# A decoder layer with stick-breaking attention: a pair's two heads taken together, K's low products on half of the rows, and two smaller reorderings

## Chip, cores and metric

The kernel runs on one core of a Trainium2 chip. The metric is the device time of one execution in microseconds (us). A core has a tensor engine (PE, whose weight loads are listed apart as PEld), VectorE (DVE), ScalarE (ACT), GpSimd (POOL) and SyncE (SP), which here issues most DMAs.

## The reference, cut to what matters

With a depth of 1 there is one layer: 1024 positions, a width of 1024, 16 heads of 64, everything in 32-bit floats.

```python
def stick_breaking_attention(h, w_in, w_out):
    """A[t,s] = sigmoid(z_ts) * prod_{s<j<t} (1 - sigmoid(z_tj)), s < t."""
    ...
    z = jnp.einsum('bhqd,bhkd->bhqk', qb, k).astype(jnp.float32) * scale
    log_fail = jnp.where(causal, jax.nn.log_sigmoid(-z), 0.0)
    after = lax.cumsum(log_fail, axis=3, reverse=True) - log_fail
    a = jnp.where(causal, jnp.exp(jax.nn.log_sigmoid(z) + after), 0.0)
    return jnp.einsum('bhqk,bhkd->bhqd', a, v.astype(jnp.float32))
    ...

    h = h + stick_breaking_attention(rms_norm(h, norm_mix), sb_w_in, sb_w_out)
    h = h + swiglu(rms_norm(h, norm_ffn), ffn_w_in, ffn_w_out)
    h = h + sigmoid(rms_norm(h, norm_ple) @ ple_w_gate) * (p @ ple_w_proj)
    return rms_norm(h, final_norm)
```

## The kernel before

Activations lie transposed, features on the 128 partitions and positions along the free axis. Every operand of a large product is split into a high part (rounded to the engine's fast 32-bit format) and a low part, the rest; `mm3` (L126) makes three products of 128x128 by 128x512 from them: high by high, high by low, low by high. A weight tile is loaded by SP (`w_load`, L88) and split by `w_split` (L97): ACT copies the high part (L106), DVE or POOL subtracts for the low part (L108). PSUM has eight banks; two (`pj`) belong to projections, the others to the stage at hand.

**Attention** (L169 to L586). The input is loaded, split and squared, and the first pair's Q and K are projected at once (L247 to L264). Then heads go in eight pairs. `proj_steps` (L322) is a generator that yields after each of 48 steps (three matrices, two halves of 512 positions, eight contraction tiles; three products a step) and projects the next pair while the current one is in attention; for the last pair `ple_steps` (L488) takes its place, which projects the embedding and begins the output projection. `evac_q`, `evac_k` and `evac_v` (L278 to L306) empty the projection banks with DVE and ACT. Q of head A lies with its high part on rows 0 to 63 and its low part on rows 64 to 127 (`QA`); head B the other way round (`QB`). K's high part stands on both halves (`KA`, `KB`); its low part (`KLA`, `KLB`) stands on one half beside zeros written once at the start. `evac_v` makes differences of neighbouring positions of V (`dv`, L305), which `turn_v` (L308) transposes on PE; turns wait in the list `late`, which is emptied in the fourth step of each half (L331).

A score atom `s_atom` (L398) is one head and 128 query positions: for each piece of up to 512 key positions (`pieces`, L392) it makes two products into a bank of the tag `zt` (four banks, shared with the transposes), L407 with K's high parts and L408 with its low parts; ACT takes the sigmoid (L410), and DVE a scan over the reversed axis (L417), which is issued behind the next score atom. A value atom `a_atom` (L424) is one head, one window of 512 queries and 128 keys: up to four transposes (L430) into a bank, ACT's high part `ah` (L439), DVE's low part `al` (L440), and, three atoms later (`LAG`), two products with V (L450, L451). `finish` (L457) adds the two halves of the result and, after the second head, V itself, splits it and writes it to DRAM. The loop at L532 lays atoms out by hand: 32 windows (pair, head, half), the score atoms of one window among the value atoms of the window before, and after each atom as many projection steps as a share of weights says (`SHARE`, a score atom weighing `2 * (qt + 1)`). Up to here a planner orders the instructions by dependences, free buffers and the order of issue; from L650 on (`tc_manual`) the order is that of the program. The tag `qf` is a ring of three 512-column buffers for short-lived tiles.

**FFN, first half** (L843 to L914). 22 steps `k`, each with seven products `prod` (a Strassen-like scheme), sums by `add` (L634) that empty the PSUM banks, scaling by the norm (`scaled`, L828, on DVE or POOL) and the gate (`glu`, L830: ACT's sigmoid, then L833 and L834 on DVE, and a DMA to DRAM). `glu` of the second half of the positions is put off to the next step as `tail`. In the last step the first two tiles of the next stage's weights (`w_split(n_fi)`, `w_split(n_fi + 1)`) and activations (`act_split`, L622) are split as well.

**FFN, second half** (L944 to L975). For each half of the positions, 22 steps: eight `mm3`, one into each bank, the first of them into the banks that the sums above have to leave. The gated embedding and the last norm follow.

Of the kernel before, what the change touches and what calls it, by code (L numbers as in the profile page):

```python
# [14 lines left out]
P = 128  # L15
# [10 lines left out]
NA = 4  # L26
SHARE = 0.48
# [13 lines left out]
def tile_trunk(ctx: ExitStack, tc: tile.TileContext, xT, pT, gains, ident, w_qkv, w_o, w_fi, w_fo, w_g, w_p, outT):  # L41
# [54 lines left out]
    def w_split(k):  # L96
        if k < lim[0] and k in raws:  # L97
# [9 lines left out]
            eng = nc.gpsimd if k < N1 or k >= len(order) - 3 else nc.vector  # L107
# [61 lines left out]
    with ExitStack() as c1:  # L169
# [40 lines left out]
        pad = [p1.tile([P, 256], F32R, name=f"pad{k}") for k in range(2)]  # L210
        for k in range(2):
            nc.scalar.copy(pad[k][:, :P], zero)

        VF = [p1.tile([P, T + 1], F32, name=f"vf{q}") for q in range(2)]
        for q in range(2):
            nc.gpsimd.memset(VF[q][:, 0:1], 0.0)

        KLS = [[p1.tile([P, T], F32R, name=f"KL{'AB'[hd]}{q}") for hd in range(2)] for q in range(2)]
        for q in range(2):
            for hd in range(2):  # L220
                r = slice(64 - 64 * hd, 128 - 64 * hd)
                nc.gpsimd.tensor_copy(KLS[q][hd][r, :], zero[r, 0:1].to_broadcast([64, T]))

# [49 lines left out]
        def alloc_qk(pr):  # L273
            for n in ("QA", "QB", "KA", "KB"):
                setattr(prs[pr], n, p1.tile([P, T], F32R, name=f"{n}{pr}", tag=n, bufs=2))
            prs[pr].KL = KLS[pr % 2]

        def evac_q(pr, ps, h):  # L278
            o = prs[pr]
            hs = slice(h * 512, h * 512 + 512)  # L280
            q = p1.tile([P, 512], F32, name="qf", tag="qf", bufs=3)
# [6 lines left out]
        def evac_k(pr, ps, h):  # L288
            o = prs[pr]
            hs = slice(h * 512, h * 512 + 512)  # L290
            q = p1.tile([P, 512], F32, name="kf", tag="qf", bufs=3)
# [5 lines left out]
            nc.gpsimd.tensor_tensor(o.KL[0][0:64, hs], q[0:64], f(o.KA[0:64, hs]), op=ALU.subtract)  # L297
            nc.gpsimd.tensor_tensor(o.KL[1][64:128, hs], q[64:128], f(o.KB[64:128, hs]), op=ALU.subtract)

        def evac_v(pr, ps, h):  # L300
            t0 = h * 512
            v = VF[pr % 2]
            nc.vector.tensor_tensor(v[:, t0 + 1:t0 + 513], ps, rstd[:, t0:t0 + 512], op=ALU.mult)
            dv = p1.tile([P, 512], F32, name="dv", tag="qf", bufs=3)
            nc.vector.tensor_tensor(dv, v[:, t0:t0 + 512], v[:, t0 + 1:t0 + 513], op=ALU.subtract)  # L305
            return dv  # L306
# [15 lines left out]
        def proj_steps(pr, sels=(0, 1, 2)):  # L322
            for sel in sels:
# [38 lines left out]
        def evac_first(h):  # L362
            o = prs[0]
            hs = slice(h * 512, h * 512 + 512)
            q = p1.tile([P, 512], F32, name="qf", tag="qf", bufs=3)
            nc.vector.tensor_tensor(q, qk0[0][h], rstd[:, hs], op=ALU.mult)
            k = p1.tile([P, 512], F32, name="kf", tag="qf", bufs=3)
            nc.vector.tensor_tensor(k, qk0[1][h], rstd[:, hs], op=ALU.mult)
            for hd, (Q, K) in enumerate(((o.QA, o.KA), (o.QB, o.KB))):
# [7 lines left out]
                eng.tensor_tensor(o.KL[hd][a, hs], k[a], f(K[a, hs]), op=ALU.subtract)  # L377
# [20 lines left out]
        def s_atom(pr, hd, qt):  # L398
# [3 lines left out]
            Q = o.QA if hd == 0 else o.QB  # L402
            K = o.KA if hd == 0 else o.KB
            a = p1.tile([P, L], F32, name=f"a{qt}", tag=f"a{qt}", bufs=1)
# [9 lines left out]
            def rest():  # L414

                back = slice(T - 1, T - L - 1 if L < T else None, -1)
                nc.vector.tensor_tensor_scan(a[:, L - 1::-1], a[:, L - 1::-1], hot[:, back], 0.0, op0=ALU.mult, op1=ALU.max)  # L417

            pend_s.append(rest)
            a_tiles[(pr, hd, qt)] = a  # L420
# [3 lines left out]
        def a_atom(pr, hd, w, kt):  # L424
# [6 lines left out]
            c0 = j0 * P  # L431
            if j0 < 3:
                ah = p1.tile([P, 512], F32R, name="ah", tag="ah", bufs=NA)
                al = p1.tile([P, 512], F32R, name="al", tag="al", bufs=NA)
                m0 = c0
            else:
                ah, al = pad
                m0, c0 = P, 256
            nc.scalar.copy(ah[:, m0:m0 + 512 - j0 * P], b[:, j0 * P:])  # L439
            nc.vector.tensor_tensor(al[:, m0:m0 + 512 - j0 * P], b[:, j0 * P:], f(ah[:, m0:m0 + 512 - j0 * P]), op=ALU.subtract)  # L440
            r0 = c0 if j0 < 3 else 0
# [3 lines left out]
            def rest():  # L445
# [4 lines left out]
                nc.tensor.matmul(ps[:, c0:], o.V[:, kt, hd, :], ah[:, r0:], start=kt == 0, stop=False)  # L450
                nc.tensor.matmul(ps[:, c0:], o.V[:, kt, hd, :], al[:, r0:], start=False, stop=last)  # L451
# [5 lines left out]
        def finish(pr, hd, w, ps):  # L457
            if hd == 0:
                stage[(pr, w)] = p1.tile([P, 512], F32, name="stg", tag="stg", bufs=2)
            st = stage[(pr, w)]  # L460
            t = p1.tile([64, 512], F32, name="avt", tag="qf", bufs=3)
            nc.scalar.copy(t, ps[64:128, :])
            nc.vector.tensor_tensor(st[64 * hd:64 * hd + 64, :], ps[0:64, :], t, op=ALU.add)
            if hd == 1:
                ws = slice(w * 512, w * 512 + 512)
                nc.vector.tensor_tensor(st, st, VF[pr % 2][:, w * 512 + 1:w * 512 + 513], op=ALU.add)
                if pr < NPAIR - 1:
                    hl = p1.tile([P, 2, 512], F32R, name="hl", tag="hl", bufs=1)
                    h, l = hl[:, 0, :], hl[:, 1, :]
# [7 lines left out]
                if pr < NPAIR - 1:  # L477
                    nc.sync.dma_start(spill[pr][:, :, ws], f(hl))
# [636 lines left out]
```

## Time and profile before

| | |
|---|---|
| median of 3 runs | 1397.57 us (1396.01 to 1397.66) |
| profiled execution | 1397.2 us, span 1395.4 us |
| PE busy | 1359.3 us, 97% of the span |
| DVE / ACT / POOL busy | 1006.8 / 609.2 / 406.4 us |
| mean granted clock of PE | 0.993 of full speed |

The span reaches from the first to the last instruction; the execution's time has some 2 us around it. Products are pipelined: a product's listed length is a model and longer than the distance to the next one's start, so costs on PE are read from starts. The trace's times count from the span's start.

### The profile page before, as it was taken

To read this page: it belongs to the slowest core of one execution; us is meant where nothing else is said; L and a number is where in the kernel's file an instruction comes from. 1 tells how busy PE (TensorE), PEld (TensorE's weight loads), DVE (VectorE), ACT (ScalarE), POOL (GpSimd) and SP (SyncE) were. 2 spreads that over 40 slices of the span, in tenths; PEclk is the share of its full clock that TensorE was granted. 3 is DMA by queue.
4 is the path that set the end of the run, shared out by engine and by line. 5 is a ranking of instruction groups with operands and counts; after the bars stand their busy time and mean duration, and the time that the engine had idled before them with its cause. 6 is when DMAs were issued, how large, how long until landed. Compare 5 with 4: busy or idle time off the path is not lost. (4 is left out here: it accounts for less than half of the span.)

```text
span 1395.4 us, 17612 instructions
## 1 busy us (share of the span) xinstructions
PE 1359.3 (97%) x6620; PEld 1135.1 (81%) x6620; DVE 1006.8 (72%) x1305; ACT 609.2 (44%) x1082; POOL 406.4 (29%) x280
## 2 busy tenths in 40 slices
PE   8899999999999999999999999999999999999996
PEld 6788888888888878878888888888877888888896
DVE  6778788787887875677888888888884336645775
ACT  6555665655566664443232323222322223433333
POOL 2221322312222501234445444545440000301321
PEclk9999999999999999999999999999999999999998
DMA  5101111111111571442221222221235445555123
GB/s 188 41 31 46 46 46 46 46 34 43 46 46 61 182 263 46 162 146 79 91 85 58 84 91 91 91 71 66 91 106 188 138 156 208 168 175 181 31 71 104
DMA packets 55509, 137.54 MB, mean 99 GB/s; under 512 B 6016, under 2 KB 10496, under 8 KB 55424
## 3 DMA queue, kind: packets, MB, share of 16 engines
q1 hardware_dynamic: 53136, 128.82, 27.1%
q0 software_dynamic: 2016, 7.34, 1.5%
q8 instruction: 52, 0.85, 0.3%
q14 instruction: 33, 0.27, 0.1%
q10 hardware_dynamic: 272, 0.26, 0.1%
HBM read 104.94 MB, written 31.46 MB: 98 GB/s over the span
## 5 line engine op out<-in xcount | busy, mean ns | idle before, releaser
L417 DVE TENSOR_TENSOR_SCAN a<-a,hot 128x128 f32<-128x128 f32 (+7 forms) x128 | 191.7, 1515 | 29.4 <-ACT a L410 28.9
L108 DVE TENSOR_TENSOR wlo<-wraw,whi 128x1024 fp32r<-128x1024 f32 x57 | 71.6, 1256 | 124.4 <-ACT whi L106 124.3
L106 ACT CAST whi<-wraw 128x1024 fp32r<-128x1024 f32 x84 | 88.2, 1051 | 165.2 <-PE b_m L128 144.8
L108 POOL TENSOR_TENSOR wlo<-wraw,whi 128x1024 fp32r<-128x1024 f32 x27 | 67.6, 2509 | 297.6 <-ACT whi L106 141.5
L127 PE MATMUL b_pj<-xh,whi 128*128 128x512 f32 x352 | 141.1, 401 | 0.0
L129 PE MATMUL b_pj<-xh,wlo 128*128 128x512 f32 x352 | 139.1, 395 | 0.4 <-POOL wlo L108 0.4
L128 PE MATMUL b_pj<-xl,whi 128*128 128x512 f32 x352 | 138.5, 393 | 0.0
L440 DVE TENSOR_TENSOR al<-b_tp,ah 128x512 fp32r<-128x512 f32 (+2 forms) x160 | 93.1, 599 | 51.3 <-ACT ah L439 50.9
L439 ACT CAST ah<-b_tp 128x512 fp32r<-128x512 f32 (+2 forms) x160 | 81.9, 522 | 78.4 <-PE b_tp L430 77.5
L410 ACT ACTIVATE a<-b_z 128x128 f32<-128x128 f32 (+2 forms) x192 | 86.8, 490 | 56.5 <-PE b_z L408 55.5
L127 PE MATMUL b_m<-act,whi 128*128 128x512 f32 x264 | 104.0, 394 | 3.5 <-DVE u L634 3.4
L129 PE MATMUL b_m<-act,wlo 128*128 128x512 f32 x264 | 103.8, 393 | 0.2 <-DVE wlo L108 0.2
L128 PE MATMUL b_m<-act,whi 128*128 128x512 f32 x264 | 103.7, 393 | 0.0
L430 PE MATMUL b_tp<-hot,a 128*128 128x128 f32 x576 | 94.2, 272 | 2.6 <-DVE al L440 2.6
L430 PEld LDWEIGHTS b_tp<-hot,a 128*128 128x128 f32 x576 | 72.8, 140 | 25.6 <-DVE al L440 5.6
L129 PEld LDWEIGHTS b_pj<-xh,wlo 128*128 128x128 f32 x352 | 66.3, 188 | 16.3 <-POOL wlo L108 0.5
L128 PEld LDWEIGHTS b_pj<-xl,whi 128*128 128x128 f32 x352 | 66.5, 189 | 9.2
L127 PEld LDWEIGHTS b_pj<-xh,whi 128*128 128x128 f32 x352 | 66.5, 189 | 9.1
L450 PE MATMUL b_av<-ah,V 128*128 128x512 f32 (+2 forms) x160 | 70.7, 442 | 0.0
L941 POOL TENSOR_TENSOR acc<-acc,sq 128x512 f32<-128x512 f32 x10 | 17.6, 1758 | 161.4 <-ACT sq L939 160.7
L832 ACT ACTIVATE sg<-u 128x512 f32<-128x512 f32 x22 | 13.9, 632 | 111.2 <-issue 86.4
L127 PEld LDWEIGHTS b_m<-act,whi 128*128 128x128 f32 x264 | 50.1, 190 | 15.1 <-DVE u L634 4.2
(3039 smaller groups left out, 3746.9 us busy)
## 6 DMA issues: line engine op xcount, KB each, us to landing
fraw<-w_fi SPq DMA_DIRECT2D x44, 512.0 KB, 4.1
wraw<-w_fo SPq DMA_DIRECT2D x44, 512.0 KB, 3.6
wraw<-w_qkv SPq DMA_DIRECT2D x22, 512.0 KB, 3.6
araw<-act SPq DMA_DIRECT2D x44, 256.0 KB, 3.9
h<-h SPq DMA_DIRECT2D x32, 256.0 KB, 3.7
sp<-hl SPq DMA_DIRECT2D x14, 512.0 KB, 3.0
act<-u SPq DMA_DIRECT2D x22, 256.0 KB, 2.2
act<-c SPq DMA_DIRECT2D x22, 256.0 KB, 2.6
```

What stands on the lines that cost most here:

```text
L106: nc.scalar.copy(hi[:, :n, :], t[:, :n, :])
L108: eng.tensor_tensor(lo[:, :n, :], t[:, :n, :], f(hi[:, :n, :]), op=ALU.subtract)
L127: nc.tensor.matmul(ps, whi, xhi, start=first, stop=False)
L128: nc.tensor.matmul(ps, whi, xlo, start=False, stop=False)
L129: nc.tensor.matmul(ps, wlo, xhi, start=False, stop=last)
L410: nc.scalar.activation(a[:, c0:c0 + e], z[:, :e], AF.Sigmoid, scale=-SCALE)
L417: nc.vector.tensor_tensor_scan(a[:, L - 1::-1], a[:, L - 1::-1], hot[:, back], 0.0, op0=ALU.mult, op1=ALU.max)
L430: nc.tensor.transpose(b[:, j * P:(j + 1) * P], a[:, kt * P:(kt + 1) * P], idn)
L439: nc.scalar.copy(ah[:, m0:m0 + 512 - j0 * P], b[:, j0 * P:])
L440: nc.vector.tensor_tensor(al[:, m0:m0 + 512 - j0 * P], b[:, j0 * P:], f(ah[:, m0:m0 + 512 - j0 * P]), op=ALU.subtract)
L450: nc.tensor.matmul(ps[:, c0:], o.V[:, kt, hd, :], ah[:, r0:], start=kt == 0, stop=False)
L941: eng.tensor_tensor(acc3[:, hs], acc3[:, hs], s, op=ALU.add)
```

## The change

**Two heads together.** A score atom now takes both heads of a pair. For each piece it makes both heads' products with K's high parts on all 128 rows, into two banks, and then both heads' products with K's low parts, each on 64 rows only: head A on rows 0 to 63, head B on rows 64 to 127. One tile `KL` per pair holds both low parts without zeros. The two scans of an atom are issued together. There are 16 windows (pair, half) instead of 32, the value atoms of both heads follow each other, and a score atom's weight is `3 * (qt + 1)`. To make room, the zeroed tiles `pad` and `KLS` go (POOL writes zeros beside the last key tile's part instead), V is kept in tiles of 513 columns with a first column that POOL fills, the output's high and low parts pass through the ring `qf`, which has four buffers, and are written by two DMAs instead of one, and the DMA scratch space is cut.

**First pair.** The turns of V of pair 0 are no longer taken up in the first half of the next pair's first matrix.

**Between the FFN's halves.** The low parts of the first two weight tiles of the second half are made on POOL and earlier, and the last step's scaling and gating (now on DVE throughout) is put off until after steps 1 and 2 of the second half.

```diff
+QF = 4
-            eng = nc.gpsimd if k < N1 or k >= len(order) - 3 else nc.vector
+            eng = nc.gpsimd if k < N1 or n_fi <= k < n_fi + 2 or k >= len(order) - 3 else nc.vector
...
-            nc.gpsimd.tensor_tensor(o.KL[0][0:64, hs], q[0:64], f(o.KA[0:64, hs]), op=ALU.subtract)
-            nc.gpsimd.tensor_tensor(o.KL[1][64:128, hs], q[64:128], f(o.KB[64:128, hs]), op=ALU.subtract)
+            nc.gpsimd.tensor_tensor(o.KL[0:64, hs], q[0:64], f(o.KA[0:64, hs]), op=ALU.subtract)
+            nc.gpsimd.tensor_tensor(o.KL[64:128, hs], q[64:128], f(o.KB[64:128, hs]), op=ALU.subtract)
...
-                        if kt == 3:
+                        if kt == 3 and (pr > 1 or sel or h):
                             while late:
                                 late.pop(0)()
...
-        def s_atom(pr, hd, qt):
+        def s_atom(pr, qt):
...
             for c0, n in pieces(L):
-                z = zb()
-                nc.tensor.matmul(z[:, :n], Q[:, qs], K[:, c0:c0 + n], start=True, stop=False)
-                nc.tensor.matmul(z[:, :n], Q[:, qs], o.KL[hd][:, c0:c0 + n], start=False, stop=True)
+                zz = [zb(), zb()]
+                for z, (Q, K) in zip(zz, hds):
+                    nc.tensor.matmul(z[:, :n], Q[:, qs], K[:, c0:c0 + n], start=True, stop=False)
+
+                for hd, (z, (Q, K)) in enumerate(zip(zz, hds)):
+                    r = slice(64 * hd, 64 * hd + 64)
+                    nc.tensor.matmul(z[:, :n], Q[r, qs], o.KL[r, c0:c0 + n], start=False, stop=True)
                 e = min(n, L - c0)
-                nc.scalar.activation(a[:, c0:c0 + e], z[:, :e], AF.Sigmoid, scale=-SCALE)
+                for a, z in zip(aa, zz):
+                    nc.scalar.activation(a[:, c0:c0 + e], z[:, :e], AF.Sigmoid, scale=-SCALE)
...
+                for a in aa:
+                    nc.vector.tensor_tensor_scan(a[:, L - 1::-1], a[:, L - 1::-1], hot[:, back], 0.0, op0=ALU.mult, op1=ALU.max)
...
+            if c0 < m0:
+                nc.gpsimd.tensor_copy(ah[:, c0:m0], zero)
+                nc.gpsimd.tensor_copy(al[:, c0:m0], zero)
...
-                    nc.sync.dma_start(spill[pr][:, :, ws], f(hl))
+                    nc.sync.dma_start(spill[pr][:, 0, ws], f(h))
+                    nc.sync.dma_start(spill[pr][:, 1, ws], f(l))
...
-        wins = [(pr, hd, w) for pr in range(NPAIR) for hd in range(2) for w in range(2)]
+        wins = [(pr, w) for pr in range(NPAIR) for w in range(2)]
...
-            elif len(A) == 8:
-                atoms = [S[0], S[1], A[0], A[1], A[2], S[2], A[3], A[4], S[3], A[5], A[6], A[7]]
+            elif len(A) == 16:
+                atoms = [S[0], S[1]] + A[:4] + [S[2]] + A[4:8] + [S[3]] + A[8:]
             else:
-                atoms = [S[0], S[1], A[0], S[2], A[1], S[3], A[2], A[3]]
+                atoms = [S[0], A[0], S[1], A[1], A[2], S[2], A[3], S[3]] + A[4:]
...
             if k == NFF - 1:
+                w_split(n_fi)
                 act_split(0)
-                w_split(n_fi)
...
-            if k:
+            if 0 < k < NFF - 1:
                 scaled(c22, 1, nc.gpsimd)
                 scaled(q1, 0)
             todo[5]()
             if k == NFF - 1:
+                w_split(n_fi + 1)
                 act_split(1)
...
-        tail()
+        def rest_0(q1=q1, u2=u2):
+            scaled(q1, 0)
+            scaled(u2, 0)
+            glu(NFF - 1, 0, q1, u2)
+
+        def rest_1(u4=u4, c22=c22):
+            scaled(u4, 1)
+            scaled(c22, 1)
+            glu(NFF - 1, 1, u4, c22)
+
+        rests = [rest_0, rest_1]
...
             else:
                 tail.append((wh, wl, a))
+            if k and rests:
+                rests.pop(0)()
```

## Rows read from the trace of the kernel before

**Rows 1.** The page's first part: busy us (share of the span) x instructions.

```profile
PE 1359.3 (97%) x6620; PEld 1135.1 (81%) x6620; DVE 1006.8 (72%) x1305; ACT 609.2 (44%) x1082; POOL 406.4 (29%) x280
```

**Rows 2.** Table by stage: window, length, busy us (instructions) of the five engines named.

```profile
core 0: us, PE busy (x) PEld busy (x) DVE busy (x) ACT busy (x) POOL busy (x), PEclk, DMA share, GB/s
46.97:55.27 8.30, 4.37 (x16) 3.26 (x15) 6.14 (x6) 2.98 (x5) 3.62 (x2) 0.79 0.22 63
174.00:233.00 59.00, 58.37 (x314) 48.97 (x313) 47.93 (x59) 35.57 (x71) 15.26 (x9) 1.00 0.13 42
1039.54:1055.47 15.93, 12.19 (x37) 8.50 (x36) 12.14 (x17) 4.29 (x6) 2.95 (x2) 0.79 0.26 86
1056.00:1350.00 294.00, 294.00 (x1378) 246.74 (x1377) 148.81 (x190) 104.79 (x149) 36.76 (x23) 1.00 0.43 146
```

**Rows 3.** Waits of PE, whole span: waiter <- releaser: total us, times, longest.

```profile
PE b_tp L314 <- DVE dv L305: 5.3, 3, 2.1
...
PE b_m L127 <- DVE u L634: 3.4, 2, 3.2
...
PE b_pj L127 <- ACT plt L513: 1.7, 1, 1.7
```

**Rows 4.** PE in order of time, first pair: start, length, line, operation [idle before].

```profile
46.97 0.39 PE L129 MATMUL b_pj<-xh,wlo 128*128 128x512 f32 x1
...
51.91 1.12 PE L314 MATMUL b_tp<-hot,dv 128*128 128x128 f32 x4 [2.13 <-DVE dv L305]
52.68 0.78 PE L127 MATMUL b_pj<-xh,whi 128*128 128x512 f32 x1
...
55.27 0.40 PE L127 MATMUL b_pj<-xh,whi 128*128 128x512 f32 x1
```

**Rows 5.** PE in order of time, from the FFN's first half into its second.

```profile
1039.54 0.39 PE L127 MATMUL b_m<-act,whi 128*128 128x512 f32 x1
...
1049.09 0.79 PE L127 MATMUL b_m<-act,whi 128*128 128x512 f32 x1 [3.23 <-DVE u L634]
...
1055.47 0.40 PE L127 MATMUL b_pj<-act,whi 128*128 128x512 f32 x1
```

**Rows 6.** DVE in order of time, ahead of the longest of these waits.

```profile
1046.61 0.69 DVE L834 TENSOR_TENSOR u<-q,u 128x512 f32<-128x512 f32 x1 [1.17 <-POOL u L828]
1047.21 1.22 DVE L108 TENSOR_TENSOR wlo<-wraw,whi 128x1024 fp32r<-128x1024 f32 x1
```

**Rows 7.** POOL in order of time, same stretch.

```profile
1041.79 1.30 POOL L828 TENSOR_TENSOR c<-c,rstd 128x512 f32<-128x512 f32 x1 [8.59 <-DVE c L634]
```

**Rows 8.** PE in order of time: score products of 256 and 512 columns.

```profile
57.32 0.28 PE L407 MATMUL b_z<-KA,QA 128*128 128x256 f32 x1
57.44 0.28 PE L408 MATMUL b_z<-KLA,QA 128*128 128x256 f32 x1
...
58.14 0.40 PE L407 MATMUL b_z<-KA,QA 128*128 128x512 f32 x1
58.37 0.40 PE L408 MATMUL b_z<-KLA,QA 128*128 128x512 f32 x1
```

**Rows 9.** All of L408 for head A: count, ns min/median/max, first and last start, forms.

```profile
L408 PE MATMUL b_z<-KLA,QA x96: 277/337/397, 57.4 to 494.5; 128*128 128x384 f32 x24, 128*128 128x512 f32 x24, 128*128 128x256 f32 x16, 128*128 128x320 f32 x16
```

**Rows 10.** PE in order of time: into transposes and out of them.

```profile
240.44 0.39 PE L129 MATMUL b_pj<-xh,wlo 128*128 128x512 f32 x1
240.67 0.38 PE L430 MATMUL b_tp<-hot,a 128*128 128x128 f32 x2
240.81 0.48 PE L450 MATMUL b_av<-ah,V 128*128 128x512 f32 x1
241.13 0.39 PE L451 MATMUL b_av<-al,V 128*128 128x512 f32 x1
```

**Rows 11.** Weight loads in order of time, same place.

```profile
240.78 0.19 PEld L450 LDWEIGHTS b_av<-ah,V 128*128 128x128 f32 x1
240.89 0.19 PEld L451 LDWEIGHTS b_av<-al,V 128*128 128x128 f32 x1
```

**Rows 12.** Groups of DVE by shape, 57 to 530 us: busy us, mean ns.

```profile
L417 DVE TENSOR_TENSOR_SCAN a<-a,hot 128x1024 f32<-128x1024 f32 x16 | 37.2, 2328 | 7.3 <-ACT a L410 7.3
```

More of the change, by code (lines that the diff above doesn't have):

```diff
@@ L209, in tile_trunk @@
         nc.scalar.activation(warm, ones, AF.Sigmoid)
[L210 to L222, printed above, removed]
         w0h = [wp.tile([P, KT, P], F32R, name=f"whi_s{s}", tag="whi", bufs=2) for s in range(2)]
@@ L273, in alloc_qk @@
         def alloc_qk(pr):
-            for n in ("QA", "QB", "KA", "KB"):
+            for n in ("QA", "QB", "KA", "KB", "KL"):
                 setattr(prs[pr], n, p1.tile([P, T], F32R, name=f"{n}{pr}", tag=n, bufs=2))
-            prs[pr].KL = KLS[pr % 2]
+            prs[pr].v = {}
         def evac_q(pr, ps, h):
@@ L416, in rest @@
                 back = slice(T - 1, T - L - 1 if L < T else None, -1)
-                nc.vector.tensor_tensor_scan(a[:, L - 1::-1], a[:, L - 1::-1], hot[:, back], 0.0, op0=ALU.mult, op1=ALU.max)
+                for a in aa:
+                    nc.vector.tensor_tensor_scan(a[:, L - 1::-1], a[:, L - 1::-1], hot[:, back], 0.0, op0=ALU.mult, op1=ALU.max)
             pend_s.append(rest)
-            a_tiles[(pr, hd, qt)] = a
+            for hd in range(2):
+                a_tiles[(pr, hd, qt)] = aa[hd]
         avs = {}
@@ L430, in a_atom @@
                 nc.tensor.transpose(b[:, j * P:(j + 1) * P], a[:, kt * P:(kt + 1) * P], idn)
[L431 to L441, printed above, removed]
+            m0 = j0 * P
+            c0 = min(m0, 256)
+            ah = p1.tile([P, 512], F32R, name="ah", tag="ah", bufs=NA)
+            al = p1.tile([P, 512], F32R, name="al", tag="al", bufs=NA)
+            if c0 < m0:
+                nc.gpsimd.tensor_copy(ah[:, c0:m0], zero)
+                nc.gpsimd.tensor_copy(al[:, c0:m0], zero)
+            nc.scalar.copy(ah[:, m0:], b[:, m0:])
+            nc.vector.tensor_tensor(al[:, m0:], b[:, m0:], f(ah[:, m0:]), op=ALU.subtract)
             while len(pend_a) >= LAG:
@@ L449, in rest @@
                 last = kt == 4 * w + 3
-                nc.tensor.matmul(ps[:, c0:], o.V[:, kt, hd, :], ah[:, r0:], start=kt == 0, stop=False)
-                nc.tensor.matmul(ps[:, c0:], o.V[:, kt, hd, :], al[:, r0:], start=False, stop=last)
+                nc.tensor.matmul(ps[:, c0:], o.V[:, kt, hd, :], ah[:, c0:], start=kt == 0, stop=False)
+                nc.tensor.matmul(ps[:, c0:], o.V[:, kt, hd, :], al[:, c0:], start=False, stop=last)
                 if last:
@@ L533, in tile_trunk @@
             atoms = []
-            S = [("s",) + wins[i][:2] + (4 * wins[i][2] + j,) for j in range(4)] if i < len(wins) else []
+            S = [("s", wins[i][0], 4 * wins[i][1] + j) for j in range(4)] if i < len(wins) else []
             A = []
             if i:
-                pr, hd, w = wins[i - 1]
-                A = [("a", pr, hd, w, kt) for kt in range(4 * w + 4)]
+                pr, w = wins[i - 1]
+                A = [("a", pr, hd, w, kt) for hd in range(2) for kt in range(4 * w + 4)]
             if not S:
@@ L553, in tile_trunk @@
                 done = 0
-            tot = sum(2 * (a[3] + 1) if a[0] == "s" else 4 - max(a[4] - 4 * a[3], 0) for a in atoms)
+            tot = sum(3 * (a[2] + 1) if a[0] == "s" else 4 - max(a[4] - 4 * a[3], 0) for a in atoms)
             acc_w = 0
-            if i < len(wins) - 4:
-                share = (SHARE if i % 2 else 1 - SHARE) / 2
-                base = i % 4 // 2 / 2 + (i % 2) * (1 - SHARE) / 2
+            if i < len(wins) - 2:
+                share = SHARE if i % 2 else 1 - SHARE
+                base = (i % 2) * (1 - SHARE)
                 nfill = 48
             else:
-                share = SHARE_LAST
-                base = (i + 4 - len(wins)) * SHARE_LAST
+                share = 2 * SHARE_LAST
+                base = (i + 2 - len(wins)) * 2 * SHARE_LAST
                 nfill = 46
@@ L570, in tile_trunk @@
                     s_atom(*a[1:])
-                    acc_w += 2 * (a[3] + 1)
+                    acc_w += 3 * (a[2] + 1)
                 else:
```

53 lines of the change are left out of this document (29 added, 24 removed).

## The prediction, made before the changed kernel was built or run

> **What bounds the kernel now.** I read the page's first part, then a table by stage, then what the tensor engine waited for, then its instructions in order of time. The tensor engine (PE) is busy for 97% of the span [rows 1]. In the attention stage of one head pair it is busy for 58.37 of 59.00 us at full clock, in the long FFN-out stage for all of 294.00; in two short stretches it is not, and there the granted clock is 0.79 on the mean [rows 2]. Its waits are few: three on the V differences, 5.3 us; two on an FFN sum, 3.4 us; one on a copy of the embedding projection, 1.7 us [rows 3]. So a gain has two sources: products taken off PE, or these stalls with the half clock behind them. VectorE (DVE) is second, at 47.93 of 59.00 us in a pair [rows 2].
>
> The sum is made against the profiled execution: 1397.2 us, with a span of 1395.4. The median of the runs is 1397.57, so the two agree within 0.4 us. About 0.2% (2.8 us) is what a measurement of this kernel can tell from no change.
>
> **Edit 1, the end of the FFN's first half.** Today the last step's gating and scaling sit on DVE ahead of the sums that empty PSUM banks: a product of L834 waits 1.17 us for POOL's scaling, then comes the 1.22 us weight split of L108, and only then the sum for which PE waits 3.2 us [rows 3, 6]. From the first FFN-out product at 1039.54 to the 37th at 1055.47 pass 15.93 us [rows 5]; 36 products at 0.23 us (512 columns [rows 8]) need 8.3. So 7.6 us are lost: waits, and a clock that the rows show at half after the longest one (the 1049.09 product is 0.79 long, the 1055.47 one 0.40 [rows 5]). The change splits the two weights earlier and on POOL, and defers scaling and gating behind the second and third FFN-out steps. POOL is free for it: it idles 8.59 us ahead of 1041.79 [rows 7]. What is moved (four DVE scalings and four DVE products, two DMAs out on SP) lands where DVE is busy 148.81 of 294.00 us [rows 2]; the moved outputs are read about 20 steps later. I take **-7.4**, bounds -6 to -7.6.
>
> **Edit 2, V's turn of the first pair.** PE stops after 46.97, turns V at about 49.2 and again at 51.91, and is at full clock again at 55.27 [rows 4]. Of these 8.30 us, seven products at 0.23 (1.6 us) and eight transposes at 0.07 (0.6 us; two take 0.14 [rows 10]) with 0.1 behind them are work: 6.0 us are lost. The change lets the transposes wait until eleven projection steps (before: three) have been issued. The eight steps not held up are 24 products, 5.5 us, and the first scores come between, so the second DVE difference (done by about 51.9) is ready. I take **-5.7**, bounds -4 to -6.
>
> **Small ones.** The shared ring of 512-column buffers grows from three to four, which should end most of the 1.7 us wait behind the embedding copies [rows 3]; but the outputs' high and low parts, with one DMA each on SP instead of one for both, now pass through the same ring, and hold a buffer until their DMA has landed. I take **-1**, bounds 0 to -1.7. The zeroed tiles at the start go, and small POOL copies per window come instead; POOL is no bound in this stage, so I take nothing, bounds 0 to +2.
>
> **Edit 3, two heads at once.** Each score piece of a head is two products on 128 rows: with K's high parts, and with K's low halves, where half of the rows are zeros. There are 96 of the latter in each head of a pair [rows 9], 12 per pair: 256 columns twice, 320 twice, 384 three times, 448 twice, 512 three times, 4736 in all. A 256-column product starts 0.12 us after the one before, a 512-column one 0.23 [rows 8]: 0.45 ns per column. So the low products cost 4736 x 0.45 = 2.13 us per head and pair, 34.1 us over 16 heads. Afterwards those of head A use rows 0 to 63 and those of head B rows 64 to 127. If both run side by side, half is saved: 17.1 us.
>
> A bound on this: four weight loads per piece stay, and two loads in a row start 0.11 us apart [rows 11], so a pair's piece can't go below 0.44 us. That bites only at 256 columns: the saving there is 4 x 0.1175 - 0.44 = 0.03 us instead of 0.12, and about 0.14 at 320 columns. Per pair: 2 x 0.03 + 2 x 0.14 + 3 x 0.173 + 2 x 0.20 + 3 x 0.23 = 1.95 us, over eight pairs **-15.6**. (The Trainium skill, "TensorE: Matmul & The Clock Gate", LDWEIGHTS, says that a load's time goes by its columns, not its rows, so a load of half the rows is no cheaper; no row here has such a load. If it were half as long, the sum would take 17.1.)
>
> What the trace doesn't show is a product on half of the rows, nor the price of going into that form and out again, 96 times each. The nearest row is another change of form, between transposes and products: going into transposes costs nothing (240.44 to 240.67 is the usual 0.23), coming out costs 0.09 (240.81 to 241.13 is 0.32 instead of 0.23) [rows 10]. From below the price is nothing: loads already run a step ahead of their products. From above it is a drained engine: the tail of a product beyond the next start (0.40 - 0.23 = 0.17 [rows 8]) and a load that cannot go ahead (0.11 [rows 11]), 0.28 each way. I take the nearest row, 0.09 per tiled pair of products: 96 x 0.09 = **+8.6**. Edit 3 on PE then gives -15.6 + 8.6 = **-7.0**.
>
> Its other side: a piece now takes two of the four PSUM banks shared with the transposes, and scans come in twos on DVE, of up to 2.33 us each [rows 12]. The totals on DVE, ACT and in the banks stay; what is queued behind a second scan are the subtractions of L440, and PE's value products wait for them. DVE has 11 us to spare per pair [rows 2], and projection products lie behind every score step, so I take 0.1 us per pair, and one scan exposed in the last window, where only four projection steps are left and the first transposes must wait for a scan: **+3** in all, bounds 0 to one exposed scan per pair, 8 x 2.33 = 18.6.
>
> **Sum:** -7.4 - 5.7 - 1.0 - 7.0 + 3 = -18.1; 1397.2 - 18.1 = **1379** us.
>
> **The rivals.** *Free change of form:* without the 8.6 it is 1370.5, without the +3 as well 1367.5. For it: loads are issued one product ahead throughout. Chance 0.20. *Price both ways:* 2 x 0.09 each time, 17.3 us, eats the gain and leaves the two stall edits: 1388. Chance 0.13. *The halves don't run side by side:* the low products keep their 34.1 us and pay 8.6: 1379 + 15.6 = 1395, with the price both ways 1403. Against it: the two use separate rows, separate banks and no common operand. Chance 0.05.
>
> *The engine empties (slower):* each change of form lets the running product end and loads behind it. At 0.28 each way a tiled pair costs 0.56 and saves 0.16: 96 x 0.40 = +38, so 1397.2 - 11.1 + 38 = 1424. It decides from 0.14 us per change on (0.28 per tiled pair), where the 15.6 and the 11.1 of the other parts are both used up. For it: the change makes 192 such switches in a stage that PE alone bounds, so nothing hides them. Against it: the one switch that the rows show costs 0.09 [rows 10]. (The Trainium skill, "TensorEngine Tiling (Array Packing)", Key Properties, says that a change of the tiling mode drains the engine, which speaks against this change; no row has one.) Chance 0.15. *Scans in twos:* one exposed per pair instead of the +3: 1379 + 15.6 = 1395. Against it: a stage with 11 us spare on DVE. Chance 0.05.
>
> **How the numbers follow.** The forecast has the rest, 0.42, with some microseconds either way from the bounds of edits 1 and 2. The range 1368 to 1399 takes in the free change but for its end, the price both ways and the scans; it leaves out the emptying engine and little else, under 2 in 10. Faster by over 0.2%, below 1394.8: 0.42 + 0.20 + 0.13 and some of the halves and scans, 0.78. Slower, above 1400.4: 0.15 and a little, 0.17. Within: 0.05.
>
> **What would show it.** In the changed profile the half-row products of a piece should start within some hundredths of a microsecond of each other; 0.23 apart at 512 columns means that they don't overlap. The start of the next full product, less the column time, gives the price of leaving the form; the first half-row start, that of entering. PE should run on past 1039 without half clock, and without stops at V's first turn. In the waits, PE behind DVE's L440 or the scans of L417 would speak for the scans. I am wrong if a tiled pair's price is not near 0.09 us; the rest rests on stalls that the rows hold.

## The result, and the profile after

The changed kernel takes 1439.91 us (median; 1438.60 to 1440.43) against 1397.62 us of the kernel before beside it: a ratio of 1.0301 with the interval [1.0284, 1.0319]. It is 42 us slower, where a time 18 us lower was forecast. Its profiled execution has a span of 1437.7 us. All ratios here are to the kernel before, measured anew beside each group of runs, with a 95% interval; its median was 1396.1 to 1397.6 us, so a difference of up to 1.5 us between runs of different groups says nothing.

The page's first part, as in [rows 1]:

```profile
PE 1393.8 (97%) x6620; PEld 1128.5 (78%) x6620; DVE 1007.8 (70%) x1305; ACT 608.5 (42%) x1080; POOL 468.8 (33%) x354
```

PE has as many instructions as before and the same share of the span, and is busy 34.5 us longer. So this row says that products take longer, by themselves or by a lower clock; whether something also holds PE up must be read from the stages. Line numbers are those of each kernel itself: V's difference is L305 before and L301 after, the scores' low products are L408 and L407, DVE's subtraction `al` is L440 and L441. The table by stage (columns as in [rows 2]), of the kernel before: from the first score product to the last value product, and the first half of the FFN's output stage (1058 products).

```profile
57.32:537.73 480.41, 472.52 (x2522) 396.04 (x2521) 386.31 (x466) 288.28 (x569) 120.66 (x80) 1.00 0.20 68
1039.54:1286.71 247.17, 243.43 (x1058) 200.01 (x1056) 115.48 (x127) 85.12 (x112) 16.14 (x10) 0.99 0.51 171
```

The same two stages of the changed kernel:

```profile
51.07:588.50 537.43, 512.20 (x2532) 392.11 (x2531) 392.49 (x468) 289.23 (x571) 184.31 (x158) 0.98 0.19 62
1089.50:1328.83 239.33, 239.33 (x1058) 198.17 (x1057) 113.15 (x126) 83.67 (x110) 14.20 (x9) 1.00 0.53 174
```

The first score product starts 6.2 us earlier (51.10 instead of 57.32 [rows 8]) and the FFN's output stage is 7.8 us shorter: these are edits 2 and 1. The attention stage is 57.0 us longer. Length less PE's busy time is PE's idle time: it went from 7.9 to 25.2 us, +17.3; the busy time went up by 39.7 us with ten instructions more (eight of them the transposes of V's first turn, which edit 2 moves into the stage). Three readings go further. First the waits of PE over the whole span, as in [rows 3] (`b_tp` is a bank for transposes, `b_z` for scores, `b_av` for value products, `b_pj` for projections):

```profile
PE b_tp L310 <- DVE dv L301: 14.0, 7, 2.0
PE b_pj L128 <- ACT plt L514: 6.9, 2, 4.0
...
PE b_z L403 <- DVE al L441: 4.1, 8, 1.5
```

The V differences (5.3 before) and the embedding copies (1.7 before) now hold PE for 20.9 us. Second the granted clock behind such waits, two rows of the table by stage (the clock is the third figure from the end):

```profile
163.50:166.90 3.40, 3.40 (x15) 3.00 (x14) 1.93 (x4) 1.50 (x4) 0.33 (x2) 0.50 0.02 5
...
532.20:535.60 3.40, 3.21 (x8) 2.54 (x9) 0.69 (x1) 1.32 (x4) 0.00 (x0) 0.51 1.04 385
```

There are six such stretches of half clock in the attention stage of this execution, 20.5 us together: five behind waits for V's differences, one behind a wait for a copy. The kernel before has none in its stage. PE is busy for 20.2 of the 20.5 us and needs about twice the time there (512-column products start 0.42 apart instead of 0.23, in rows further down), so about 10 of the 39.7 us are the clock (an estimate from these stretches). Third PE in order of time, where two 320-column pieces of both heads follow each other:

```profile
200.59 0.31 PE L403 MATMUL b_z<-KA,QA 128*128 128x320 f32 x1
200.74 0.31 PE L403 MATMUL b_z<-KB,QB 128*128 128x320 f32 x1
200.98 0.41 PE L407 MATMUL b_z<-KL,QA 64*128 64x320 f32 x1
200.98 0.41 PE L407 MATMUL b_z<-KL,QB 64*128 64x320 f32 x1
201.32 0.41 PE L403 MATMUL b_z<-KA,QA 128*128 128x320 f32 x1
201.57 0.31 PE L403 MATMUL b_z<-KB,QB 128*128 128x320 f32 x1
201.81 0.41 PE L407 MATMUL b_z<-KL,QA 64*128 64x320 f32 x1
201.82 0.41 PE L407 MATMUL b_z<-KL,QB 64*128 64x320 f32 x1
202.16 0.50 PE L128 MATMUL b_pj<-xh,whi 128*128 128x512 f32 x1
202.49 0.39 PE L129 MATMUL b_pj<-xl,whi 128*128 128x512 f32 x1
```

The first column is the start. Two full products of 320 columns start 0.15 us apart. The two half-row products start together, so the overlap is there. But from a full product to the first half-row one it is 0.24 us, about 0.095 more than the columns; from the half-row pair to the next full product 0.34, about 0.195 more; and the product behind that one starts 0.25 later instead of 0.145, another 0.105. At 512 columns the last step reads the same: 202.16 to 202.49 is 0.33 instead of 0.23. One excursion into the half-row form costs 0.38 to 0.4 us (0.29 where transposes follow, which don't show the last 0.105), and the pair saves 0.145.

### The profile page after: what moved, and what is told of

It is laid out like the page before. It is cut to its first block, busy times and chain, and to the rows that moved or that the text cites. A ratio compares the mean times of both kernels' runs of the same rounds, so it can differ in the third digit from the quotient of the medians.

```text
span 1437.7 us, 17828 instructions
## 1 busy us (share of the span) xinstructions
PE 1393.8 (97%) x6620; PEld 1128.5 (78%) x6620; DVE 1007.8 (70%) x1305; ACT 608.5 (42%) x1080; POOL 468.8 (33%) x354
## 4 chain that ended last, share of the span: by engine, by line
PE 87%; DVE 6%; ACT 3%; issue 2%; DMA 1%; POOL 0%; SPq 0%; DVEq 0%; ACTq 0%; POOLq 0%
PE b_m L128 15%; PE b_m L130 15%; PE b_m L129 15%; PE b_pj L128 10%; PE b_pj L129 9%; PE b_pj L130 9%; PE b_tp L432 4%; DVE a L418 3%; PE b_av L451 2%; PE b_av L450 2%; PE b_z L403 2%; PE b_z L407 2%; PE b_tp L310 1%; DVE stg L466 1%; ACT ah L440 0%
## 5 line engine op out<-in xcount | busy, mean ns | idle before, releaser
L418 DVE TENSOR_TENSOR_SCAN a<-a,hot 128x256 f32<-128x256 f32 (+7 forms) x128 | 189.2, 1512 | 46.0 <-ACT a L410 45.8
L441 DVE TENSOR_TENSOR al<-b_tp,ah 128x512 fp32r<-128x512 f32 x192 | 101.4, 550 | 71.4 <-ACT ah L440 69.4
L128 PE MATMUL b_pj<-xh,whi 128*128 128x512 f32 x352 | 146.3, 416 | 0.0
L109 POOL TENSOR_TENSOR wlo<-wraw,whi 128x1024 fp32r<-128x1024 f32 x29 | 73.8, 2551 | 187.9 <-ACT whi L107 117.9
L440 ACT CAST ah<-b_tp 128x512 fp32r<-128x512 f32 x192 | 90.2, 480 | 70.6 <-PE b_tp L432 66.5
L410 ACT ACTIVATE a<-b_z 128x384 f32<-128x384 f32 (+4 forms) x192 | 83.5, 489 | 54.6 <-PE b_z L407 52.7
L432 PE MATMUL b_tp<-hot,a 128*128 128x128 f32 x576 | 97.5, 280 | 0.0
L450 PE MATMUL b_av<-ah,V 128*128 128x512 f32 x192 | 83.1, 433 | 0.0
L128 PEld LDWEIGHTS b_pj<-xh,whi 128*128 128x128 f32 x352 | 66.7, 190 | 20.2 <-issue 9.9
L451 PE MATMUL b_av<-al,V 128*128 128x512 f32 x192 | 67.6, 352 | 0.2 <-DVE al L441 0.2
L833 ACT ACTIVATE sg<-u 128x512 f32<-128x512 f32 x22 | 13.9, 632 | 108.5 <-issue 86.4
```

The source lines that it names most:

```text
L109: eng.tensor_tensor(lo[:, :n, :], t[:, :n, :], f(hi[:, :n, :]), op=ALU.subtract)
L128: nc.tensor.matmul(ps, whi, xhi, start=first, stop=False)
L432: nc.tensor.transpose(b[:, j * P:(j + 1) * P], a[:, kt * P:(kt + 1) * P], idn)
L440: nc.scalar.copy(ah[:, m0:], b[:, m0:])
L441: nc.vector.tensor_tensor(al[:, m0:], b[:, m0:], f(ah[:, m0:]), op=ALU.subtract)
L450: nc.tensor.matmul(ps[:, c0:], o.V[:, kt, hd, :], ah[:, c0:], start=kt == 0, stop=False)
```

## The experiments

Two theories stood against each other. **A**: the loss is the change of form, a price per excursion that PE alone shows. **B**: the loss is on the other side, in what changes when both heads go through an atom together: banks, scans in twos, the order of V's turns, the shared ring. The experiments take the parts apart, and then the parts of the parts.

**The two reorderings alone.** The kernel before, with edits 1 and 2 and nothing of edit 3.

```diff
+eng = nc.gpsimd if k < N1 or n_fi <= k < n_fi + 2 or k >= len(order) - 3 else nc.vector
+if kt == 3 and (pr > 1 or sel or h):
+rests = [rest_0, rest_1]   # the last step's scaling and gating, after steps 1 and 2
```

> The kernel before with the two reorderings alone: V's first turn later, and the earlier weight split with the late scaling and gating between the FFN's halves. Heads stay apart. If the two stalls carry what I took for them (5.7 and 7.4 us), and the changed kernel's trace shows their gain (first scores 6.2 us earlier, FFN's second half 7.9 us shorter), 1397.6 - 14 = 1384 us. If the gain in the changed kernel came from its other edits, less: 1390 or more.

Measured: 1385.53 us, 0.9915 [0.9893, 0.9937], or -11.9 us. The attention stage is 1.2 us longer than before, with the eight transposes that edit 2 moves into it, and PE is at full clock:

```profile
51.07:532.65 481.58, 473.55 (x2530) 396.84 (x2529) 388.34 (x469) 288.77 (x571) 120.96 (x81) 1.00 0.20 69
```

So both stall edits hold, and by the difference of the ratios edit 3 costs 54 us. This version is faster than both kernels, and no later one beat it.

**Heads together, K's low part on all rows.** The changed kernel, with one line altered; the order on every engine stays. (It adds a term that doesn't belong there, the low part of one head's Q times the low part of the other head's K; it is at rounding level.)

```diff
-nc.tensor.matmul(z[:, :n], Q[r, qs], o.KL[r, c0:c0 + n], start=False, stop=True)
+nc.tensor.matmul(z[:, :n], Q[:, qs], o.KL[:, c0:c0 + n], start=False, stop=True)
```

> The changed kernel, but K's low products use all 128 rows again (Q's high and low part on one side, both heads' low parts of K on the other; the extra product of two low parts is at rounding level). Every engine's order stays that of the changed kernel. Theory A, the price of going into half-row form and out: about 110 groups at 0.095 + 0.195 + 0.105 = 0.395 us (43.5 us) go, 81 overlaps of 0.17 (13.9 us) go too: 1440 - 30 = 1410 us. Theory B, taking heads together with its scans in twos and its banks is the cause, and half rows are nearly free: 1440 to 1454 us.

Measured: 1420.41 us, 1.0167 [1.0148, 1.0186]. Neither theory: 19.5 us lie in the half rows, 35 in what comes with heads together. The stage, and PE's waits in it:

```profile
50.90:567.50 516.60, 482.07 (x2532) 398.20 (x2531) 386.62 (x468) 287.58 (x571) 184.60 (x158) 0.99 0.19 64
```

```profile
PE b_tp L310 <- DVE dv L301: 14.0, 7, 2.0
PE b_z L403 <- DVE al L441: 10.3, 14, 1.9
PE b_pj L128 <- ACT plt L514: 5.9, 3, 3.8
...
PE b_z L403 <- ACT a L410: 4.0, 8, 0.8
```

Against the two reorderings alone the stage is 35.0 us longer: 26.5 us idle (34.5 instead of 8.0) and 8.5 us in longer products, at a mean granted clock of 0.99 instead of 1.00: two stretches of half clock, 6.8 us, are worth 3.4 of the 8.5. Against this run the changed kernel's stage has 30.1 us more of busy time and 9.3 us less of idle time. Of the 30.1, some 6.7 are the clock (20.5 us of half clock against 6.8), so the half rows themselves cost 23 us on PE. A part comes back because a slower PE waits less: for `al` 4.1 instead of 10.3, for `a` nothing instead of 4.0. Why the same seven waits for V's differences are followed by half clock five times there and once here, the runs don't show.

**Half rows, heads apart.** The kernel before, with one line altered: K's low products on 64 rows, nothing overlaps, the order on every engine stays.

```diff
-Q[:, qs], o.KL[hd][:, c0:c0 + n]
+Q[64 * hd:64 * hd + 64, qs], o.KL[hd][64 * hd:64 * hd + 64, c0:c0 + n]
```

> The kernel before with one line changed: K's low products use 64 rows instead of 128 (the zeros on the other half are left out), one head at a time, so that nothing overlaps. Same order on every engine, 192 products in half-row form, each by itself. Theory A: 192 x 0.395 = 76 us more, 1473 us. If a change of form costs what my prediction took, 0.09 per group: 17 us more, 1415. If it is free and the trouble is elsewhere: 1398.

Measured: 1459.82 us, 1.0448 [1.0426, 1.0471]: +63.7 us for 192 excursions, 0.33 each. PE in order of time, and the stage:

```profile
251.75 0.28 PE L407 MATMUL b_z<-KA,QA 128*128 128x256 f32 x1
251.96 0.38 PE L408 MATMUL b_z<-KLA,QA 64*128 64x256 f32 x1
252.27 0.38 PE L407 MATMUL b_z<-KA,QA 128*128 128x256 f32 x1
252.58 0.38 PE L408 MATMUL b_z<-KLA,QA 64*128 64x256 f32 x1
252.89 0.66 PE L430 MATMUL b_tp<-hot,a 128*128 128x128 f32 x4
```

```profile
58.01:602.20 544.19, 543.33 (x2522) 395.26 (x2521) 388.33 (x466) 300.53 (x569) 119.96 (x80) 1.00 0.18 60
```

A 256-column step takes 0.21 into the form, and 0.31 out of it, where it took 0.12 [rows 8]. The stage is at full clock, so its figures are free of the clock: 70.8 us more of busy time, 0.37 per excursion, and 7.0 us less of idle time. This is the price by itself, near the expected 0.395 (where transposes follow, the last 0.105 is missing); the time rose by less, because 7 us of waits were covered.

**V's turn later.** The changed kernel, with the turns of V put off by four projection steps.

```diff
-if kt == 3 and (pr > 1 or sel or h):
+if kt == 7 and (pr > 1 or sel or h):
```

> The changed kernel with V's turns taken up in the eighth step of a projection half instead of the fourth. The changed kernel's PE waits seven times 2.0 us (14 us) for the V differences, which stand behind a 2.3 us scan on DVE, and runs at half clock behind five of these waits (about 1.7 us each). If the scans in twos cause these waits, four more steps (2.8 us) hide them: 1440 - 14 - 8 = 1418 us. If the waits only move to another instruction, 1435 to 1440 us.

Measured: 1422.60 us, 1.0184 [1.0164, 1.0204], -17.3 us against the changed kernel. The 14.0 us on `dv` are gone from PE's waits; the copies lead them, with 7.6. The half clock in the stage falls from 20.5 to 6.8 us, worth 6.8; but the half-row products now stand in 117 excursions with 75 overlaps instead of 110 with 82, which costs 7 x 0.37 + 7 x 0.17 = 3.8. Together that makes 17.0.

Why the turn came late is read in the changed kernel, on DVE, POOL and PE in order of time:

```profile
158.66 0.67 DVE L299 TENSOR_TENSOR vf<-b_pj,rstd 128x512 f32<-128x512 f32 x1
159.24 2.28 DVE L418 TENSOR_TENSOR_SCAN a<-a,hot 128x1024 f32<-128x1024 f32 x1
161.43 0.67 DVE L301 TENSOR_TENSOR dv<-vf 128x512 f32<-128x512 f32 x1
```

```profile
159.39 2.11 POOL L295 COPY vf<-vf 128x1 f32<-128x1 f32 x1 [3.70 <-DVE vf L299]
```

```profile
162.25 0.63 PE L310 MATMUL b_tp<-hot,dv 128*128 128x128 f32 x4 [1.99 <-DVE dv L301]
...
164.32 0.63 PE L128 MATMUL b_pj<-xh,whi 128*128 128x512 f32 x1
164.74 0.63 PE L129 MATMUL b_pj<-xl,whi 128*128 128x512 f32 x1
```

The second head's scan of 2.28 us has got between V's scaling (L299) and V's difference (L301). That is so in all seven pairs that wait, and always in the first half of the positions; in the kernel before, from its second pair on, the difference starts 0.1 us behind the scaling each time. The new copy of one column on POOL is not what delays it: the copy serves the second half's tile, and the second half's difference follows its scaling at once. It is itself held up: beside a scan it takes 2.11 us, seven times, and ends within 0.02 us of the scan's end; at 45.02, with no scan on DVE, it took 0.53 us. The transposes wait 1.99 us, and afterwards 512-column products start 0.42 apart instead of 0.23, at the lower of the clock's two levels (1.2 GHz).

**Fewer excursions.** The changed kernel, in an atom first the full products of both its pieces, then the half-row products.

```diff
+todo_z = [(c0, n, [zb(), zb()]) for c0, n in pieces(L)]
+for c0, n, zz in todo_z: ...   # full products of all pieces
+for c0, n, zz in todo_z: ...   # half-row products of all pieces
+for c0, n, zz in todo_z: ...   # sigmoids
```

> The changed kernel with a score atom's full products of both pieces first and the half-row products of both pieces behind them. The 192 half-row products then stand in 80 groups instead of 110, for four banks held at a time. If the price is per change of form (0.38 us per group, as the half rows taken one at a time showed), 30 groups fewer are 11 us: 1440 - 11 = 1429 us. If it is per half-row product, or if banks are what counts, 1440 us or more.

Measured: 1429.23 us, 1.0235 [1.0219, 1.0251], -10.7 us. That is the expected time, but by luck: the parts weren't those expected. There are 80 excursions instead of 110, at 0.37 worth 11 us. Inside a group of more than two there is a cost again (PE in order of time):

```profile
202.41 0.44 PE L407 MATMUL b_z<-KL,QA 64*128 64x384 f32 x1
202.41 0.44 PE L407 MATMUL b_z<-KL,QB 64*128 64x384 f32 x1
202.69 0.34 PE L407 MATMUL b_z<-KL,QA 64*128 64x384 f32 x1
```

The third starts 0.28 after the first, where 384 columns take 0.173. With 30 groups of three or four, some 3 us of the 11 go again. The half clock in the stage falls from 20.5 to 10.2 us; PE is busy for 20.2 and 6.6 of them, which gives 6.8 us of busy time back. And the waits were exchanged, V's against the banks':

```profile
PE b_z L403 <- DVE al L442: 9.6, 15, 2.2
...
PE b_tp L310 <- DVE dv L301: 6.4, 7, 0.9
...
PE b_z L403 <- ACT a L411: 3.2, 7, 0.7
```

**Full rows, V's turn later** (both one-line edits above).

> The changed kernel without half rows (all 128 rows in K's low products) and with V's turns in the eighth step. What is left against the two reorderings alone (1420.4 - 1385.5 = 35 us) is then heads together without the V waits. Theory: 14 us of waits and 3.4 us at half clock go, 1403 us; the 14 us of waits for banks (behind L441 and L410) stay. Rival: the waits move elsewhere, 1418 us or more.

Measured: 1406.44 us, 1.0067 [1.0051, 1.0083]. V's turn is worth 14.0 us here. Its waits are gone, but of what they had covered a part came up at the copies (5.9 before):

```profile
PE b_pj L128 <- ACT plt L514: 9.5, 2, 6.7
```

Against the run with half rows and the later turn, PE's busy time in the stage is 479.0 instead of 508.2 us, with nearly the same cost of the clock: 117 excursions at 0.37 less 75 overlaps at 0.17 make 30.5 for these 29.2, so the price holds here too.

**Grouped, V's turn later.**

> The changed kernel with both: half-row products of both pieces behind the full ones (87 groups; 117 with the later turn alone) and V's turns in the eighth step. If gains add up: 1422.6 - 30 x 0.38 = 1411 us. If four banks held at a time cost what the fewer changes of form give, 1420 to 1425 us.

Measured: 1426.53 us, 1.0212 [1.0195, 1.0229], 2.7 us less than grouped, and 3.9 more than with the later turn alone, though there are 87 excursions instead of 117. The intervals of these two runs overlap a little, so it is no gain; the second expectation (1420 to 1425) came near. The two gains don't add: grouping had already left only 6.4 of V's 14.0 us, and with the later turn the fewer excursions are paid for by PE's waits behind `al` and `a`, which go from 4.1 to 12.7 us.

**Buffers of their own for the embedding copies.** Full rows, V's turn later, and `plt` taken from buffers that are free by then, not from the ring `qf`.

```diff
-t = p1.tile([P, 512], F32, name="plt", tag="qf", bufs=QF)
+t = p1.tile([P, T], F32, name="plt", tag=("KA", "KB", "KL")[(8 * m4 + 2 * m + h) % 3], bufs=2)[:, :512]
```

> As the run with full rows and the later turn, but the embedding projection's copies (plt, L514) go through buffers that the last pair leaves free (tags KA, KB, KL) instead of the ring of four, which the outputs' two parts hold until their DMAs have landed. If that ring is what PE waits for in the last pair (three waits, 5.9 to 7.6 us, with half clock behind the longest), 6 to 9 us less than that run. If not, the same time.

Measured: 1400.48 us, 1.0027 [1.0015, 1.0039], -6.0 us. In the changed kernel, ACT in order of time shows for what the copies waited:

```profile
525.88 0.58 ACT L514 COPY plt<-b_pj 128x512 f32<-128x512 f32 x1 [3.94 <-POOL ol L476]
...
531.75 0.58 ACT L514 COPY plt<-b_pj 128x512 f32<-128x512 f32 x1 [5.29 <-DMA sp<-ol]
```

The ring's buffers were held by the output's low parts, once until POOL had made one and once until its DMA had landed. What is left in PE's waits of this run:

```profile
PE b_z L403 <- DVE al L441: 10.2, 14, 1.9
...
PE b_av L450 <- POOL ah L438: 4.3, 1, 4.3
PE b_z L403 <- ACT a L410: 4.0, 8, 0.8
```

It is 15 us above the two reorderings alone. 14.2 us are waits for a PSUM bank behind these two lines, where the two reorderings alone have 4.8 us of such waits (behind L440). The wait of 4.3 us is none for a bank, and came up when the 9.5 us behind the copies were gone: the value product of L450 reads the zeros that POOL now writes beside the last key tile's part, and POOL came to them late, in order of time:

```profile
490.63 2.37 POOL L109 TENSOR_TENSOR wlo<-wraw,whi 128x1024 fp32r<-128x1024 f32 x1
...
494.15 1.33 POOL L438 CAST ah<-zero 128x128 fp32r<-128x128 f32 x1
```

Behind it PE runs at half clock for a while, which costs some 1.7 us.

**The same buffers in the version of the two reorderings.**

> The two reorderings alone, and the embedding projection's copies in buffers that the last pair leaves free (tags KA, KB) instead of the ring of three. In that run PE waited once, 1.6 us, for such a copy. 1385.5 - 1.6 = 1384 us if the ring was the cause; 1385.5 if it wasn't.

Measured: 1387.07 us, 0.9939 [0.9926, 0.9951], no gain: with heads apart PE waits for the copies 2.8 us in place of 1.6. The ring was short only where both heads' outputs come in a row.

**A fifth bank for scores and transposes**, taken from the two of the value products, on the version of 1400.48 us.

```diff
-tag="zt", bufs=4
+tag="zt", bufs=5
-return bank("av", 2)
+return bank("av", 1)
```

> As the run with full rows, later turn and own buffers (1400.5 us), but the banks shared by scores and transposes are five instead of four, and the value products have one instead of two. What is left there against the two reorderings alone is 15 us, of which 14 us are waits for those banks (behind L441 and L410). If four banks are too few for two heads at once, most of it goes: 1388 to 1392 us. If the single bank of the value products takes it back, 1400 us or more.

Measured: 1405.70 us, 1.0065 [1.0052, 1.0079], 5 us slower. PE's waits:

```profile
PE b_av L450 <- DVE stg L463: 16.8, 21, 3.0
...
PE b_z L403 <- DVE al L441: 0.9, 1, 0.9
```

The 14.2 us of waits for a bank became 0.9, which speaks for a lack of banks, though the new waits may have covered a part. The next head's first value product now waits until DVE has emptied the only value bank. With eight banks in all, this division of them moved the lack and didn't end it.

**Half rows on five banks.** The run before, with K's low products on 64 rows again. All 96 pairs now stay together, where the changed kernel splits 28 of its 192 half-row products off.

> As the run with five banks, but with half rows as in the change: the order on every engine is the same, with 96 groups of two half-row products, all side by side. Price 96 x 0.38 = 36.5 us, saving 17.1 us by overlap: 19 us more than with full rows, or down to 14 if the price covers waits that full rows show. If half rows gain once they always overlap, up to 17 us less.

Measured: 1412.82 us, 1.0121 [1.0107, 1.0135], +7.1. By the price it should be 96 x 0.37 = 35.5, less the overlap of 17.1 that the prediction worked out for unbounded loads, +18.4. PE's waits for value banks, for the value products' operands, for V and for banks fell from 22.7 to 12.9 us in all, the largest to

```profile
PE b_av L450 <- DVE stg L463: 12.7, 15, 2.6
```

That is 9.8 of the 11.3 us between. So even with every pair overlapped the half rows lose.

**Grouped on five banks.** The same, full products of both pieces first: 65 excursions, 31 of them with four products.

> As the run before it (five banks, half rows), with the half-row products of both pieces of an atom behind its full ones: 65 groups instead of 96, 31 of them of four. Per change of form: 31 x 0.38 = 11.8 us less, and 0.1 us more in each group of four between its two halves (the trace of the grouped run shows that): 8.7 us less than that run.

Measured: 1408.79 us, 1.0091 [1.0075, 1.0106], -4.0 us. A piece's banks are held longer by grouping, and that wait is new:

```profile
PE b_z L403 <- DVE al L442: 6.2, 7, 1.2
```

## Why the prediction was wrong, step by step

**What bounds the kernel** was read rightly: PE, with hardly a wait. What I drew from it was too kind. A DVE with 11 us to spare per pair [rows 2] can still be late by 2 us at one place, seven times, and the clock can fall behind it.

**Edits 1 and 2** were right. The FFN's stage became 7.8 us shorter (forecast 7.4), the first score product came 6.2 us earlier (5.7), and both alone gave 11.9 us of 13.1.

**The overlap of edit 3** was right, in size too: the two half-row products start together, and 82 pairs at 0.17 us give 13.9 us where 15.6 were taken. The bound on it was not. I had said that two loads in a row start 0.11 us apart and that a pair's piece can't go below 0.44 us. The weight loads in order of time, same place as above:

```profile
200.98 0.18 PEld L407 LDWEIGHTS b_z<-KL,QA 64*128 64x128 f32 x1 [0.19 <-issue]
200.98 0.18 PEld L407 LDWEIGHTS b_z<-KL,QB 64*128 64x128 f32 x1
201.32 0.19 PEld L403 LDWEIGHTS b_z<-KA,QA 128*128 128x128 f32 x1 [0.16 <-issue]
```

The loads of the two halves start together as well; a load of half the rows is listed with 0.18 us, one of all rows with 0.19. (The Trainium skill, "TensorEngine Tiling (Array Packing)", Key Properties, says that a change of the tiling mode drains the engine; the 0.37 us per excursion and the late loads here agree with that.)

**The step that failed first is the +8.6**, the price of the form. I took it from the nearest row, transposes, at 0.09 us. The same loads show why that row was the wrong neighbour. My reason for a low price was that loads run a step ahead of their products; across a change of form they don't. Each first load behind a change starts with its product, in these rows after 0.16 to 0.19 us in which the load sequencer did nothing. The 0.09 behind transposes is the like of only the last of the three parts, the 0.105 on the product behind the first. The price is 0.37 us per excursion, measured alone with heads apart, in place of 0.09; and there were 110 excursions, not 96, because with four banks the two heads' products of some pieces came apart. So 110 x 0.37 = 40.7 stands in place of 8.6, which with the overlap gives +27; the busy time rose by 30.1, of which some 6.7 are the clock, so that 23 stand against these 27. The rival of the emptying engine had the late loads, and its threshold of 0.28 per pair was passed; its price, 0.56 per pair, was too high.

**The second failure is the other side, +3 (and the ring's -1).** With full rows, heads together cost 35 us. Taken off one by one in the runs: V's turn 14.0, the ring 6.0, and 15 that remain. The fifth bank did not take these apart; by the traces 9.4 are more waits for banks (14.2 instead of 4.8), 4.3 the wait for POOL's zeros and 1.7 the clock behind it, against which 3.0 us of other waits are gone, and some 3 us stay unexplained. The ring and POOL's small copies were named in the prediction, one costed with the wrong sign and one at nothing; V's turn in the later pairs was not named. For the ring I saw that the outputs' parts would hold a buffer until their DMA had landed, and still took a gain. For V's turn I costed the scans in twos by the spare time of DVE and looked at what waits behind L440 and the scans, but not at what comes between two dependent instructions of V. What carries a bank's wait, four banks with a piece in two of them, I had mentioned and not priced. The rival of exposed scans came near this part: it had one scan of 2.33 us per pair, and seven waits of 2.0 us were measured, though for V's difference and not behind L440. Its 1395 is far off because it left the price of the form at 8.6.

**The sum.** Edit 3 was -5.0 in the forecast and is +54: 32 us by the price, 2 by the overlap, 33 by the other side, less 9 by the waits that a slower PE covers, which makes 58 of the 59 us between. With the measured busy time, +30.1 with the clock in it, in place of price and overlap, the same sum gives 61. The range ended at 1399 because I held the emptying engine to be the one case left out, and took the price of the form and the cost of the other side to be apart; both were high at once.

**What stays open.** Of the 8.5 us of longer products with full rows 3.4 are the clock; the rest is not broken up. How the price divides between an engine that drains and a load that comes late, no run separates. Nor was an eviction tried that frees the value bank sooner. That a pair of 512 columns (saving 0.23 us) by itself doesn't pay for its excursion follows from 0.37; no form of this kernel was found in which half rows pay.

## What to carry to other kernels

Two products on separate row halves do run at once, but going into that form and out again costs 0.37 us here, more than a pair of up to 512 columns saves; count excursions first, and what holding more banks for fewer of them costs. Before two streams are merged, follow each short chain of dependent instructions (here two on DVE) and ask what long instruction can now come between, and count what each shared ring and bank holds until when: the mean load of the engine doesn't show it. Take the stretches of half clock out of a difference in busy time before it is put to a cause. Gains that lie in front of a busy engine don't add: what slows the engine covers other waits, so each must be measured with the other in place.

## What was not expected of the hardware

- The price of the half-row form lies in three places: 0.095 us going in, 0.195 going out, and 0.105 on the product behind the first full one; a fourth, 0.105, comes between two half-row products on the same rows within a group. The 0.105 is no property of this form alone: 0.09 shows behind transposes [rows 10], and behind the stop of PE that ended at 526.51 in the changed kernel the second product starts 0.34 after the first instead of 0.23, at full clock.
- No load is issued ahead across the change (in the rows shown the load sequencer is idle for 0.16 to 0.19 us before it), while the loads and the products of the two halves start within 0.01 us of each other.
- A copy of one column on POOL that started beside a scan of 2.28 us on DVE took 2.11 us and ended with the scan, seven times of seven; with no scan it took 0.53 us.
